# A bidirectional RWKV-7 scan on one core: another fixed order for solve steps, triangles and the attention group's output products

## The chip, the cores and the metric

The kernel runs on one core of a Trainium2 chip. The core has engines that work side by side, each through its own list of instructions: PE (TensorE: matrix products, with PEld as its weight load), DVE (VectorE), ACT (ScalarE), POOL (GpSimd) and SP (SyncE, which here only issues DMA transfers). SBUF is the on-chip memory, PSUM the banks into which PE writes. The metric is the device time of one execution in microseconds (us). The kernel before took a median of 2341.67 us over three runs, 2338.5 to 2344.6.

## What is computed

One layer of an encoder on x of shape 1 x 1024 x 1024, float32. In the reference, cut to what matters:

```
f = swiglu(rmsnorm(h), w_gate, w_up, w_down);  h = h + 0.5 * rmsnorm(f)
z = rmsnorm(h) @ w_in                        # attention q|k|v and RWKV r|k|v|decay|rate|gate
y_att  = dilated_attention(z[..., :1536]) * attn_out_g      # 8 heads of 64, normalised per head
y_rwkv = rwkv7(z[..., 1536:])                # 8 heads of 64, forward and backward
h = h + rmsnorm(concat(y_att, y_rwkv) @ w_out)
h = h + 0.5 * rmsnorm(swiglu(rmsnorm(h)))    # second feed-forward, D_FF = 2816

def step(state, r, w, k, v, kk, kka):        # rwkv7, per token, direction and head
    sa = state @ kk
    state = state * w - outer(sa, kka) + outer(v, k)
    return state, state @ r
```

The change concerns the stage in which the RWKV recurrence runs. The attention half of the product with w_out (512 of its 1024 rows) is worked in the same stage.

## The kernel before

Stages follow each other: the first feed-forward layer; projections and attention; preparation of the scan's first blocks beside the last projections; the scan; the finish of both halves with the rest of the output product; the second feed-forward layer. Where a feed-forward, projection or output product is made, float32 operands are split in a high and a low part, and three products are summed.

The recurrence is done in chunks of 64 tokens. The 1024 tokens are eight **blocks** of 128, two chunks each, and both directions and all eight heads are worked together. For block n there are these parts, each a Python generator or function that records instructions when it is advanced:

- *Preparation* (prep_parts). For each direction, `exps` makes two exponentials on ACT (L854, L855), and `times` scales keys, rates and receptances on DVE (L865 to L869, with a copy on ACT, L866). `triangles(d, i)` makes chunk i's products of keys with queries on PE (L876, tile lp) and returns `mask`, which cuts each of two halves to its triangle on DVE (L878, into lm). `turns(d)` transposes the scaled keys on PE (L888) and ACT copies them out (L891). `store` writes the triangles' diagonal pieces to DRAM (d_x) by SP (L897).
- *Solve* (solve_parts). It loads these pieces back in another layout as X and inverts them in 31 steps. A step is a product (L936, ttmp) and a subtraction (L938, Ti) on DVE, each dependent on the one before. A transpose on DVE (L941) ends it.
- *Merge* (merge_parts). Three groups of small products on PE (L953, L959, L966) with copies on ACT between (L954, L961 and L962, L968) build the inverse of twice the size. L953 needs the transpose of the solve.
- *Chain* (chain_parts). First come copies on ACT (L1002). Then, for each chunk in turn, products with the state and the values on PE (L1014, L1027, both xu), ACT copies between them (L1017 xs, L1029 uv), products into the new state st and the output y (L999), a copy of y (L1043), and the state's update by its decay on DVE (L1049, sv). Each chunk needs the state of the one before.
- *The attended output* (attended_parts) for eight tiles of 128 tokens: a row tile yat is loaded and scaled on DVE (L1271), transposed on PE (L1280, yq), split by ACT (L1282, yah) and DVE (L1286, yal). 24 products on PE (L1259, po) in four groups of six follow, and for each half of 512 columns ACT copies the sum (L1294, yao) and issues its store. The sums have one PSUM bank. The weights woh and wol are made by `out_weights` from eight loads into two raw buffers (wor).

The solve of block m+1 and the preparation of block m+2 run beside the merge and chain of block m. `scan` advances the generators in a written order. Then `in_order` ties each instruction of PE, DVE and ACT to the one recorded before it on its engine:

```
traced = self.nc.cur_bb.bb.instructions
...
for i in traced[start:]:
    if i.engine in self.ordered:
        if i.engine in last:
            self.tc.add_manual_dep(i, last[i.engine].name, ...)
        last[i.engine] = i
```

So within the scan those three engines follow the written order exactly. The lists of SP and POOL are left to the scheduler. An iteration of the scan over m is a *period* here, and it is cut at the first L953 of its merge.

Of the kernel before, what the change touches and what calls it, by code (L numbers as in the profile page):

```python
# [10 lines left out]
F32 = mybir.dt.float32  # L11
F32R = mybir.dt.float32r
# [151 lines left out]
class _Kernel:  # L164
# [903 lines left out]
    def scan(self, blk, NB, sp, sc, eo, pm, pp, pc, pe, homes, rs_a):  # L1068
# [4 lines left out]
        none = iter(())  # L1073
        go = lambda it, k=1: [next(it, None) for _ in range(k)]
        loaded = {n: {} for n in range(2, NB)}
        P, solves = {}, {}

        def loads(n, d):
            if n < NB:
                loaded[n][d] = self.prep_loads(n, d, sp)  # L1080

        def parts(n):
            if n < NB:
                got = self.prep_parts(n, sp, pp, homes[n % 3], loaded[n])
                blk[n], P[n] = got[0], got[1:]
                P[n][0](0)

        loads(2, 0)
        parts(2)
        WA = None  # L1090
        for m in range(NB):
            merge = self.merge_parts(m, blk[m], sc, pm)
            solve = solves.pop(m + 1, none)
            k = m + 2
            exps, times, triangles, turns, store = P.pop(k, (None,) * 5)
            go(merge)
            if exps:
                times(0)
                loads(k, 1)
            if WA:  # L1100
                go(rest)
            go(merge)
            chain = self.chain_parts(m, blk[m], sc, pc)
            go(chain)
            if exps:
                mask = triangles(0, 0)
            go(solve, 3)
            if WA:
                go(rest)
            if exps:  # L1110
                mask(0)
                mask(1)
            go(merge)
            go(chain)
            go(solve, 3)
            if exps:
                mask = triangles(0, 1)
                mask(0)
                go(solve)
                mask(1)  # L1120
                exps(1)
            if WA:
                go(rest)
            go(chain, 4)
            if WA:
                go(rest)
            if exps:
                times(1)
                loads(k + 1, 0)
            else:  # L1130
                go(solve, 4)
            go(chain)
            go(solve, 2)
            go(chain)
            if exps:
                turns(0)
                mask = triangles(1, 0)
            go(solve, 2)
            if exps:
                mask(0)  # L1140
                go(solve)
                mask(1)
            go(chain, 3)
            if exps:
                mask = triangles(1, 1)
            go(chain)
            go(solve, 2)
            if exps:
                mask(0)
                go(solve)  # L1150
                mask(1)
                store()
            go(chain)
            go(solve, 2)
            go(chain)
            if exps:
                turns(1)
                solves[k] = self.solve_parts(k, sp, blk[k])
                go(solves[k])
            if WA is None:  # L1160
                WA = self.out_weights(eo, 0, self.aog)
                rest = self.attended_parts(eo, sc, pe, list(range(NT)), WA, rs_a)
                go(rest)
            parts(k + 1)
            go(solve, 8)
            go(rest, 2)
            for _ in solve:
                pass
            if m >= 5:
# [58 lines left out]
    def finish_half(self, p, psum, half, x):  # L1228
        g2w = self.load_g2(p)
        for b in self.blocks[2 * half:2 * half + 2]:  # L1230
            sg = p.tile([128, FB], F32, name="f_sg", tag="f_sg", bufs=1)
            self.load(sg, self.sg_d[:, b * FB:(b + 1) * FB])
            for g in range(2):
                self.finish_unit(p, psum, b, g, x, g2w, sg)

    def out_weights(self, p, k0, gain=None, raw=None):

# [150 lines left out]
    def run(self):  # L1388
# [5 lines left out]
        with self.top as top:  # L1394
# [97 lines left out]
            blk = {}  # L1492
            for n, cts in enumerate(([], [8, 9, 10, 11])):
                blk[n] = self.prep(n, sp, pp, (R0, R1)[n])
                for _ in self.solve_parts(n, sp, blk[n]):
                    pass
# [12 lines left out]
            rs_a = self.rstd(eo, self.ss_a.rearrange("p a b -> p (a b)"), NT * H, 1.0 / HD, EPS)  # L1509
            self.scan(blk, NB, sp, sc, eo, pm, pp, pc, pe, (R0, R1, B0), rs_a)  # L1510
            s_sr.close()
            s_pr.close()

# [140 lines left out]
```

## Time and profile before

One execution was profiled. The scan runs from about 1248 to 1594 us of it.

| quantity | value |
|---|---|
| median of three runs | 2341.67 us (2338.5 to 2344.6) |
| the profiled execution, its own time | 2348.46 us |
| its span | 2346.7 us |
| mean granted TensorE clock | 0.963 |
| PE busy over the span | 2178.5 us, 93% |
| DVE busy | 1773.7 us, 76% |
| ACT busy | 1025.0 us, 44% |
| first merge's transposes (m = 0) begin | 1248.62 us |
| merges 1 to 7 begin | 1313.28, 1353.73, 1394.46, 1435.26, 1476.12, 1523.60, 1564.23 us |
| products for the second half of the output begin | 1593.83 us |

The median and the profiled execution differ by 6.8 us, so differences are formed within the one and then carried to the other. Busy shares are means over the whole program; in the scan neither PE nor DVE is full. The granted clock is the share of full speed at which PE was let run in a stretch. Group rows give the busy time, the mean duration of one in ns, and behind the second bar the idle time ahead with what ended it.

### The profile page before, as it was taken

What the parts mean: (1) busy time and instruction counts of PE and PEld (TensorE: products, weight loads), DVE (VectorE), ACT (ScalarE), POOL (GpSimd) and SP (SyncE); (2) the same over time, 40 slices, a digit from 0 to 9 for tenths busy, and PEclk for the clock granted to TensorE, in tenths of its full rate; (3) what the DMA queues carried; (4) which work ended last, traced back from release to release, by engine and by line L of the source; (5) the groups of instructions that cost most, each with busy time, mean ns of one, the idle gap of its engine ahead of it and who ended that gap; (6) DMA issues with size and microseconds to landing.
All of it is one profiled execution on the core that took longest, in us unless ns stands there. A gap on an engine that the chain in (4) does not pass through costs nothing. (4 is left out here: it accounts for less than half of the span.)

```text
span 2346.7 us, 41372 instructions
## 1 busy us (share of the span) xinstructions
PE 2178.5 (93%) x15556; PEld 1755.7 (75%) x15556; DVE 1773.7 (76%) x2893; ACT 1025.0 (44%) x1925; POOL 540.9 (23%) x673
## 2 busy tenths in 40 slices
PE   7999999999999998999997578779889999999998
PEld 5788888888877676777776466566678888887887
DVE  7999999865676344777767677646999999996566
ACT  5323323354676403676544444345442323235453
POOL 2344343400000011312212111122024443442000
PEclk9999999999999999999987889889989999999999
DMA  5354544486652515644377545436534544447665
GB/s 145 125 183 145 175 154 165 167 269 192 220 185 99 192 51 152 183 151 149 102 186 189 159 132 144 143 111 240 168 107 166 173 156 165 163 155 266 201 189 192
DMA packets 346700, 387.74 MB, mean 165 GB/s; under 512 B 73474, under 2 KB 249346, under 8 KB 346500
## 3 DMA queue, kind: packets, MB, share of 16 engines
q1 hardware_dynamic: 294928, 271.71, 38.2%
q0 software_dynamic: 31216, 100.73, 11.5%
q10 hardware_dynamic: 20356, 12.66, 1.8%
q8 instruction: 122, 2.00, 0.4%
q14 instruction: 78, 0.64, 0.1%
HBM read 258.06 MB, written 126.94 MB: 164 GB/s over the span
## 5 line engine op out<-in xcount | busy, mean ns | idle before, releaser
L81 PE MATMUL gu<-xh,wh 128*128 128x512 f32 x704 | 277.5, 394 | 4.6 <-ACT wh L186 4.5
L186 ACT ACTIVATE wh<-raw 128x512 fp32r<-128x512 f32 (+1 forms) x273 | 168.5, 628 | 250.2 <-DVE raw L62 93.4
L81 PE MATMUL gu<-xh,wl 128*128 128x512 f32 x704 | 276.1, 392 | 0.0
L81 PE MATMUL gu<-xl,wh 128*128 128x512 f32 x704 | 276.1, 392 | 0.0
L187 DVE TENSOR_TENSOR wl<-raw,wh 128x512 fp32r<-128x512 f32 (+1 forms) x273 | 272.4, 1001 | 4.8 <-ACT wh L186 3.9
L421 PE MATMUL pd<-gl,gwh 128*128 128x512 f32 x616 | 240.4, 390 | 2.6 <-DVE gl L187 2.6
L421 PE MATMUL pd<-gh,gwh 128*128 128x512 f32 x616 | 239.5, 390 | 0.6 <-DVE row L86 0.6
L421 PE MATMUL pd<-gh,gwl 128*128 128x512 f32 x616 | 239.8, 389 | 0.2 <-DVE gwl L187 0.2
L86 DVE TENSOR_TENSOR row<-gu,row 128x512 f32<-128x512 f32 x308 | 206.8, 683 | 25.2 <-PE gu L81 22.9
L116 POOL DMA_DIRECT2D d_hid<-row x154 | 85.0, 553 | 546.9 <-DVE row L114 531.9
L187 DVE TENSOR_TENSOR gwl<-graw,gwh 128x512 fp32r<-128x512 f32 (+2 forms) x187 | 117.5, 636 | 119.7 <-ACT gwh L186 117.6
L186 ACT ACTIVATE gwh<-graw 128x512 fp32r<-128x512 f32 (+2 forms) x187 | 103.3, 555 | 178.7 <-PE pd L421 148.2
L81 PEld LDWEIGHTS gu<-xh,wh 128*128 128x128 f32 x704 | 133.5, 190 | 33.7 <-ACT wh L186 5.6
L81 PEld LDWEIGHTS gu<-xh,wl 128*128 128x128 f32 x704 | 133.4, 189 | 28.1 <-DVE wl L187 0.2
L81 PEld LDWEIGHTS gu<-xl,wh 128*128 128x128 f32 x704 | 133.5, 190 | 27.5
L421 PEld LDWEIGHTS pd<-gl,gwh 128*128 128x128 f32 x616 | 115.6, 188 | 27.9 <-DVE gl L187 4.3
L421 PEld LDWEIGHTS pd<-gh,gwh 128*128 128x128 f32 x616 | 115.5, 188 | 25.3 <-DVE row L86 1.0
L421 PEld LDWEIGHTS pd<-gh,gwl 128*128 128x128 f32 x616 | 115.6, 188 | 24.6 <-DVE gwl L187 0.6
L187 DVE TENSOR_TENSOR gl<-raw,gh 128x512 fp32r<-128x512 f32 x160 | 112.5, 715 | 26.3 <-ACT gh L186 26.1
L94 ACT ACTIVATE row<-row 128x512 f32<-128x512 f32 x44 | 27.9, 634 | 213.9 <-DVE row L86 210.2
L186 ACT ACTIVATE gh<-raw 128x512 fp32r<-128x512 f32 x160 | 98.2, 622 | 44.7 <-DMA raw<-in_ffn_w_down_dram 24.8
L145 POOL TENSOR_TENSOR ws<-ws 128x512 f32<-128x512 f32 x88 | 114.7, 1304 | 1.2
(364 smaller groups left out, 5171.6 us busy)
## 6 DMA issues: line engine op xcount, KB each, us to landing
d_hid<-row POOLq DMA_DIRECT2D x154, 256.0 KB, 2.5
graw<-d_hid SPq DMA_DIRECT2D x132, 256.0 KB, 2.9
raw<-in_ffn_w_gate_dram SPq DMA_DIRECT2D x88, 256.0 KB, 3.2
raw<-in_ffn_w_up_dram SPq DMA_DIRECT2D x88, 256.0 KB, 3.3
ws<-in_ffn_w_down_dram SPq DMA_DIRECT2D x88, 256.0 KB, 4.1
d_ws<-ws POOLq DMA_DIRECT2D x88, 256.0 KB, 2.3
raw<-d_ws SPq DMA_DIRECT2D x88, 256.0 KB, 2.7
raw<-in_ffn_w_down_dram SPq DMA_DIRECT2D x66, 256.0 KB, 3.9
```

The costliest lines, as they stand in the source:

```text
L81: self.K.nc.tensor.matmul(ps, a[:, k, :], b[:, k, :], start=(k == 0 and i == 0), stop=(k == 3 and i == 2))
L86: add = lambda o, x: V.tensor_tensor(o, ps, x, op=OP.add)
L94: A.activation(y[:, 0], y[:, 0], AF.Silu)
L116: put = lambda n, y: G.dma_start(self.hid[n - 1, j // 2], y)
L145: G.tensor_tensor(o, a, b, op=OP.subtract)
L186: self.nc.scalar.activation(h, src, AF.Copy)
L187: (eng or self.nc.vector).tensor_tensor(l, src, h, op=OP.subtract)
L421: T.matmul(ps[x], a[:, ts], b, start=(m == 0 and k == 0), stop=(m == NM - 1 and k == 2))
```

## The change

No arithmetic is added or taken away, and tile shapes are the same. The order in which `scan` advances the generators is rewritten:

- The solve of block 1 moves from beside the last projections into the start of the scan. There it is mixed with the preparation of block 2 (the third block). Both directions of block 2's triangles now stand ahead of merge 0. Before, the first direction was under way in merge 0 and the second between its chunks.
- The attention group's reciprocal root (rstd) moves from ahead of the scan into iteration 0. A new generator `attended_weights` makes the output weights one pair at a time between the pieces of chain 0, in place of one run after it. The solve of block 2 begins there as well and has done 20 of its 31 steps by the end of iteration 0.
- In iterations 1 to 5 `times` of the first direction stands ahead of the merge. Each of two masks is followed by a solve step (`masks`). Of a tile's four groups of products only the last stays behind the merge, while the transposes and three groups stand behind the chain, ahead of the next merge. Iteration 3 takes one more whole tile; before, the additional tiles were in iterations 5 and 6.
- Iterations 6 and 7 are written out on their own. In 6, 13 solve steps stand ahead of the first chunk's state update on DVE, and the last tile's products stand ahead of merge 7.

```
+        def masks(mask, solve):
+            for par in range(2):
+                mask(par)
+                go(solve)
...
+        solve = self.solve_parts(1, sp, blk[1])
+        go(solve, 9)
         loads(2, 0)
         parts(2)
...
+        masks(triangles(1, 0), solve)
+        masks(triangles(1, 1), solve)
+        for _ in solve:
+            pass
+        store()
+
+        merge, chain, solve = begin(0)
+        weights = self.attended_weights(eo, W)
+        go(weights)
+        go(merge)
+        turns(1)
+        go(merge)
+        go(chain)
...
+        for m in range(1, NB - 2):
+            merge, chain, solve = begin(m)
             k = m + 2
...
+            times(0)
             go(merge)
+            loads(k, 1)
             go(merge)
             go(chain)
+            mask = triangles(0, 0)
+            go(solve, 4)
+            masks(mask, solve)
+            go(merge)
+            go(chain)
+            masks(triangles(0, 1), solve)
+            exps(1)
+            go(rest)
+            go(chain)
+            times(1)
+            loads(k + 1, 0)
+            go(chain, 4)
             go(solve, 3)
+            mask = triangles(1, 0)
             go(chain)
+            go(solve, 3)
+            masks(mask, solve)
+            go(chain, 5)
+            go(solve, 4)
+            go(chain)
+            mask = triangles(1, 1)
             go(solve, 2)
+            masks(mask, solve)
+            store()
+            solving(k)
+            go(rest)
+            turns(0)
+            turns(1)
             go(solve, 2)
+            go(rest, 4)
             parts(k + 1)
             for _ in solve:
                 pass
+            if m == 3:
+                go(rest, 6)
             blk.pop(m)
...
+    def attended_weights(self, p, W):
+
+        for k in range(4):
+            hl = []
+            for dh in range(2):
+                r = p.tile([128, 512], F32, name="wor", tag="wor", bufs=2)
+                self.load(r, self.io["w_out"][0][k * 128:(k + 1) * 128, dh * 512:(dh + 1) * 512])
...
+            yield
+            for h, l, r in hl:
+                self.nc.scalar.activation(h, r, AF.Copy, scale=self.aog[:, k:k + 1])
+                self.nc.vector.scalar_tensor_tensor(l, r, self.aog[:, k:k + 1], h, op0=OP.mult, op1=OP.subtract)
+            W.append([(h, l) for h, l, r in hl])
```

What this does to the engines' lists shows at three places. In the changed kernel the lines behind scan are 66 higher: L1325 is L1259 of before (po), L1346 is L1280 (yq), L1337 is L1271 (yat).

First, PE in a middle period, around its merge; po is a product of the attended output, lp a triangle, pa the merge. Before, each of the merge's three pieces has a group of six po behind it (one such group is shown):

```order
L888 MATMUL bp<-ident,bk 128x64 x16
L1280 MATMUL yq<-ident,yat 128x128 x4
L953 MATMUL pa<-ident,X 32x32 x64
L1259 MATMUL po<-woh,yah 128x512
L1259 MATMUL po<-wol,yah 128x512
L1259 MATMUL po<-woh,yal 128x512
```

In the changed kernel, the same place:

```order
L876 MATMUL lp<-pr,bk 128x128 x8
L1346 MATMUL yq<-ident,yat 128x128 x4
L888 MATMUL bp<-ident,bk 128x64 x32
L1325 MATMUL po<-woh,yah 128x512
L1325 MATMUL po<-wol,yah 128x512
L1325 MATMUL po<-woh,yal 128x512
L953 MATMUL pa<-ident,X 32x32 x64
L959 MATMUL pa<-X,lm 32x32 x32
L876 MATMUL lp<-pr,bk 128x128 x8
L966 MATMUL pa<-tt_12003,am 32x32 x32
```

The three po rows stand there six times in all, eighteen products, and all now precede the merge, whose pieces follow each other with triangles alone between them.

Second, DVE in a middle period: the masks of the first direction (lm) among the two operations of each solve step (ttmp, Ti). Before:

```order
L878 TENSOR_TENSOR lm<-lp,k_tri 128x512 x2
L936 TENSOR_TENSOR ttmp<-X,Ti 128x56
L938 TENSOR_TENSOR Ti<-Ti,ttmp 128x28x2
L936 TENSOR_TENSOR ttmp<-X,Ti 128x81
L938 TENSOR_TENSOR Ti<-Ti,ttmp 128x27x3
L936 TENSOR_TENSOR ttmp<-X,Ti 128x78
L938 TENSOR_TENSOR Ti<-Ti,ttmp 128x26x3
L878 TENSOR_TENSOR lm<-lp,k_tri 128x512
```

In the changed kernel:

```order
L878 TENSOR_TENSOR lm<-lp,k_tri 128x512
L936 TENSOR_TENSOR ttmp<-X,Ti 128x81
L938 TENSOR_TENSOR Ti<-Ti,ttmp 128x27x3
L878 TENSOR_TENSOR lm<-lp,k_tri 128x512
L936 TENSOR_TENSOR ttmp<-X,Ti 128x78
L938 TENSOR_TENSOR Ti<-Ti,ttmp 128x26x3
L878 TENSOR_TENSOR lm<-lp,k_tri 128x512
L936 TENSOR_TENSOR ttmp<-X,Ti 128x100
L938 TENSOR_TENSOR Ti<-Ti,ttmp 128x25x4
```

Where two masks stood in a row and three steps behind them, mask and step now take turns.

Third, PE at the start of the scan (vt is the transpose of the last values, L640, xu the first product of the chain). Before:

```order
L953 MATMUL pa<-ident,X 32x32 x64
L640 MATMUL vt<-ident,us 128x128 x8
L640 MATMUL vt<-ident,vrev 128x128 x8
L959 MATMUL pa<-X,lm 32x32 x32
L876 MATMUL lp<-pr,bk 128x128 x8
L966 MATMUL pa<-tt_12073,am 32x32 x32
```

In the changed kernel:

```order
L640 MATMUL vt<-ident,vrev 128x128 x4
L876 MATMUL lp<-pr,bk 128x128 x7
L888 MATMUL bp<-ident,bk 128x64 x16
L876 MATMUL lp<-pr,bk 128x128 x16
L953 MATMUL pa<-ident,X 32x32 x64
L888 MATMUL bp<-ident,bk 128x64 x16
L959 MATMUL pa<-X,lm 32x32 x32
L966 MATMUL pa<-tt_12003,am 32x32 x32
L1014 MATMUL xu<-sv,lm 64x64 x16
```

All triangles of the third block, both directions, now stand ahead of L953 of merge 0.

More of the change, by code (lines that the diff above doesn't have):

```diff
@@ L1091, in scan @@
-        for m in range(NB):
-            merge = self.merge_parts(m, blk[m], sc, pm)
-            solve = solves.pop(m + 1, none)
+        exps, times, triangles, turns, store = P.pop(2)
+        go(solve, 5)
+        times(0)
+        loads(2, 1)
+        go(solve, 4)
+        masks(triangles(0, 0), solve)
+        masks(triangles(0, 1), solve)
[3 more added lines that the diff above has]
+        times(1)
+        loads(3, 0)
+        masks(triangles(1, 0), solve)
+        masks(triangles(1, 1), solve)
@@ L1094, in scan @@
+        go(chain, 5)
+        go(solve, 8)
+        go(weights)
+        go(chain)
+        go(solve, 2)
+        rest = self.attended_parts(eo, sc, pe, list(range(NT)), W, rs_a)
+        go(weights)
+        go(rest)
+        parts(3)
+        go(rest)
+        go(solve, 3)
+        go(rest, 4)
+        go(solve, 3)
+        solves[2] = solve
+        blk.pop(0)
+        for m in range(1, NB - 2):
+            merge, chain, solve = begin(m)
             k = m + 2
-            exps, times, triangles, turns, store = P.pop(k, (None,) * 5)
+            exps, times, triangles, turns, store = P.pop(k)
+            times(0)
@@ L1096, in scan @@
             go(merge)
[L1097 to L1112, printed above, removed]
+            loads(k, 1)
             go(merge)
@@ L1134, in scan @@
[L1134 to L1137, printed above, removed]
-            go(solve, 2)
[L1139 to L1163, printed above, removed]
+            mask = triangles(0, 0)
+            go(solve, 4)
+            masks(mask, solve)
+            go(merge)
+            go(chain)
@@ L1173, in scan @@
+        go(solve, 3)
+        go(merge)
+        go(rest)
+        go(chain)
+        go(solve, 2)
+        go(chain, 5)
+        go(solve, 13)
+        go(chain)
+        go(chain, 5)
+        for _ in solve:
+            pass
+        go(chain)
+        for _ in rest:
+            pass
+        merge, chain, solve = begin(NB - 1)
+        go(merge, 2)
+        go(chain)
+        go(merge)
+        for _ in chain:
             pass
```

64 lines of the change are left out of this document (37 added, 27 removed).

## Prediction

> **What bounds the kernel now.** I first read the busy time by stretch, cut at the starts of the eight merges (the first transposes, L953). Columns: stretch (us), its length, then busy time with instruction counts on PE, PEld, DVE, ACT and POOL, the granted clock, the DMA share and GB/s.
>
> ```profile
> 1265.20:1313.28 48.08, 25.79 (x528) 23.14 (x532) 19.61 (x35) 23.70 (x40) 9.38 (x18) 0.68 0.62 165
> 1313.28:1353.73 40.45, 30.36 (x718) 25.46 (x718) 31.07 (x90) 18.98 (x34) 4.78 (x9) 0.88 0.56 152
> 1353.73:1394.46 40.73, 30.63 (x718) 25.52 (x718) 30.30 (x88) 18.37 (x33) 6.57 (x12) 0.88 0.53 144
> 1394.46:1435.26 40.80, 30.70 (x718) 25.53 (x718) 30.31 (x88) 18.38 (x33) 6.57 (x12) 0.88 0.52 144
> 1435.26:1476.12 40.86, 30.76 (x718) 25.60 (x719) 30.31 (x88) 18.38 (x33) 6.58 (x12) 0.88 0.54 143
> 1476.12:1523.60 47.48, 39.92 (x745) 32.03 (x745) 30.84 (x87) 18.31 (x33) 6.57 (x11) 0.88 0.45 135
> 1523.60:1564.23 40.63, 31.65 (x646) 25.31 (x645) 21.41 (x70) 13.78 (x25) 12.28 (x17) 0.92 0.48 147
> 1564.23:1594.29 30.06, 25.10 (x616) 19.18 (x616) 9.83 (x16) 20.43 (x37) 2.08 (x3) 0.89 0.15 46
> ```
>
> Four periods are alike, 40.45 to 40.86 us, and in each both PE and DVE are busy some 30 us: neither fills it. The fourth row is the period that I then followed along its chain of waits (start, length, what):
>
> ```profile
> 1394.46 1.93 PE pa L953 x128
> ...
> 1411.04 1.58 PE po L1259 x6
> ...
> 1421.28 0.69 DVE lm L878
> ...
> 1432.55 0.23 DVE Ti L938
> ...
> 1435.26 0.75 PE pa L953 x39
> ```
>
> PE carries the chain to 1421.28, DVE from there to the next merge. Each waits for the other once a period. The groups of the same period (busy, mean ns, then the idle time ahead and its releaser) price that:
>
> ```profile
> L878 DVE TENSOR_TENSOR lm<-lp,k_tri 128x512 f32<-128x512 f32 x8 | 5.4, 688 | 6.2 <-PE lp L876 6.2
> L1049 DVE TENSOR_TENSOR sv<-st,gc 64x512 f32<-64x512 f32 x4 | 2.7, 687 | 1.9 <-PE st L999 1.8
> L865 DVE SCALAR_TENSOR_TENSOR bk<-ka,th_w 128x512 f32<-128x512 f32 x3 | 2.1, 687 | 0.5 <-ACT th_w L855 0.5
> L938 DVE TENSOR_TENSOR Ti<-Ti,ttmp 128x126 f32<-128x126 f32 (+22 forms) x31 | 8.0, 257 | 1.1
> L953 PE MATMUL pa<-ident,X 32*32 32x32 f32 x130 | 2.2, 237 | 19.4 <-DVE gc L861 19.4
> ```
>
> DVE waits 6.2 + 1.9 + 0.5 = 8.6 us, so its own work with the latencies between dependent steps is 40.8 - 8.6 = 32.2 us. PE's 19.4 is two waits of 9.70, since the window catches both its ends; PE's work is then 40.8 - 9.7 - 0.4 = 30.7.
>
> **The long wait also cools PE.** Single rows around it (start, length, operation, and in brackets the wait ahead):
>
> ```profile
> 1394.45 1.93 PE L953 MATMUL pa<-ident,X 32*32 32x32 f32 x128 [9.70 <-DVE gc L861]
> 1396.90 0.63 PE L1259 MATMUL po<-wol,yah 128*128 128x512 f32 x1
> 1401.74 0.39 PE L1259 MATMUL po<-wol,yah 128*128 128x512 f32 x1
> 1415.96 1.16 PE L876 MATMUL lp<-pr,bk 64*128 64x128 f32 x14 [0.41 <-ACT bt L891]
> 1564.23 1.29 PE L953 MATMUL pa<-ident,X 32*32 32x32 f32 x128
> 1198.60 1.86 PE L876 MATMUL lp<-pr,bk 64*128 64x128 f32 x13 [2.86 <-DVE lm L878]
> ```
>
> After 9.70 us of waiting the transposes take 1.93 us, where a merge behind a full PE takes 1.29; a product takes 0.63 instead of 0.39. Pipelined, products follow each other at about 0.43 and 0.235 us. Without the cold start PE's work is some 28.7 us (0.64 on the transposes, about 6 x 0.2 on products, a little on L959).
>
> **The change, part by part.** No operation is added or removed; order is all that changes. *Steady period.* Before, DVE's triangle masks stand behind PE's attended products (po), and PE's merge stands behind DVE's solve steps. In the new order only one group of six po stays between merge and chain, eighteen come in one burst behind the chain, and each mask has a solve step behind it. So DVE gets its masks' inputs in turn, and its last steps run beside the burst. I take DVE as the bound. It saves about 0.5 by masks that stand directly behind a dependent step, as these rows show:
>
> ```profile
> 1406.22 0.26 DVE L938 TENSOR_TENSOR Ti<-Ti,ttmp 128x100 f32<-128x100 f32 x1
> 1406.40 0.68 DVE L878 TENSOR_TENSOR lm<-lp,k_tri 128x512 f32<-128x512 f32 x1
> 1432.80 0.21 DVE L936 TENSOR_TENSOR ttmp<-X,Ti 128x45 f32<-128x45 f32 x1
> 1433.04 0.20 DVE L938 TENSOR_TENSOR Ti<-Ti,ttmp 128x45 f32<-128x45 f32 x1
> ```
>
> The mask starts 0.18 after a step of 0.26, a dependent step 0.24 after one of 0.21: about 0.1 for each of five new places. Three waits stay: the scaling of the next block (times) needs exponentials that now stand on ACT behind the copy of a po group, 1.9 late by my tracing (twelve po at 0.235, the copy 0.6, the issue of its store 0.34, two exponentials 1.26, against 3.4 of steps and transpose on DVE); the state update 0.7; masks 0.4. Together 32.2 - 0.5 + 3.0 = **34.7** for m = 2, 4, 5. Unseen is how PE's pieces fall, so I bound it: 31.7 if all waits vanish (32.5 with a little left), 38.2 if the burst stays cold (below). I take the middle, near the DVE sum.
>
> *m = 1* has 11 solve steps left, since 20 are done in the opening. A step is two operations of some 0.29 with their latency (L938's row: (8.0 + 1.1)/31), so 20 x 0.6 = 12 leave DVE, and PE and ACT set about **32**, near the 30.06 of the last period, which is a merge and chain without solve. *m = 3* gets the one extra attended tile: transposes 0.66, copy 0.6, difference 0.69, 24 products 5.6, a wait for the copy of the single sum 0.7 and latencies, 8.7 in all: **43.4**. Before, m = 5 paid 47.48 - 40.86 = 6.6 for the same. *m = 6* has one tile where it had two, and its solve is spread: here
>
> ```profile
> 1541.74 1.41 DVE L1049 TENSOR_TENSOR sv<-st,gc 64x512 f32<-64x512 f32 x2 [9.51 <-PE st L999]
> ```
>
> is the wait of DVE for a PE full of po. 24 x 0.235 = 5.6 leave PE and 0.5 comes as a wait: **35.5**. *m = 7* stays **30**. From merge 1 on: 32 + 34.7 + 43.4 + 34.7 + 34.7 + 35.5 = 215.0 against 250.95, that is -36.0.
>
> *Opening.* Here the change costs. The third block's second direction stands now ahead of merge 0, and its inputs come late:
>
> ```profile
> 1264.08 0.52 SPq L182 DMA_DIRECT2D in<-d_rk  x1
> 1268.05 2.08 PE L876 MATMUL lp<-pr,bk 64*128 64x128 f32 x16
> 1273.93 2.10 PE L1014 MATMUL xu<-sv,lm 64*64 64x64 f32 x32
> 1292.45 1.39 DVE L1049 TENSOR_TENSOR sv<-st,gc 64x512 f32<-64x512 f32 x2 [0.87 <-PE st L999]
> 1295.85 1.33 ACT L1249 ACTIVATE woh<-wor,c_attn_out_g 128x512 fp32r<-128x512 f32 x2
> 1310.00 0.72 ACT L1249 ACTIVATE woh<-wor,c_attn_out_g 128x512 fp32r<-128x512 f32 x1 [0.44 <-DMA wor<-in_w_out_dram]
> in<-d_rk SPq DMA_DIRECT2D x2, 512.0 KB, 4.6
> ```
>
> The load is issued at 1264.08 behind stores of the values on SP and lands 4.6 later (last row, a median), at 1268.7. Four scalings of about 0.65 bring 1271; two groups of triangles at the cold 2.08 with four masks of 0.69 bring 1279. Merge 0, begun at 1276.6, needs three cold groups of 1.9 with ACT copies of 0.6, 1.8 and 1.2, so the first value product moves from 1273.93 to about 1287, +13. Both chunks follow cold: the second state update ends near 1305 instead of 1293.8. The weight conversions stood in a run of their own, 1295.85 to 1310.7. They now go between the chunks, but with two raw buffers the last two still wait for landings, to about 1315.5. Then the first attended tile (scale 0.65, transposes 1.1, copy 0.6, difference 0.7) and 18 cold po at 0.43 = 7.7: merge 1 at **1326** instead of 1313.28, +12.7. Bounds: 1318 if the conversions hide fully in the chain, 1332 if loads on SP slip again.
>
> The sum is -36.0 + 12.7 = -23.3 on a profiled execution of 2348.46 us (its span is 2346.7): 2325.2. The median of the runs shown lies 6.8 below that execution, so I predict **2319**.
>
> **What a page says of the cold burst.** The Trainium skill, "TensorE: Matmul & The Clock Gate", section "Part 1: The HAM clock gate (the "warmup" mystery)", puts the drop to half speed at an idle window of about 3.4 us. By that rule, none of my gaps (1.5 us at most) would cool PE and the forecast stands. The row at 1198.60 is slow after only 2.86 us, so the trace is stricter than the rule.
>
> **The rivals.** (1) *The clock drops at each burst.* 18 po at 0.43 instead of 0.235 cost 3.5, in six periods 21: 2319 + 21 = about **2340**, no change. For it: the slow row after a wait of 2.86, and that the burst waits for a difference on DVE behind solve steps. Against it: 9.7 shrinks to pieces that I trace at 1.5 or less. (2) *The opening is cheaper.* If weights and attended tile fit under the chain, merge 1 starts near 1317: **2310**. For it: ACT was busy only 23.70 of 48.08 there. Against it: loads, not ACT, paced the weights. (3) *X comes late.* Each solve starts from its masked products through DRAM:
>
> ```profile
> 1422.43 0.68 DVE L878 TENSOR_TENSOR lm<-lp,k_tri 128x512 f32<-128x512 f32 x1
> 1427.74 0.53 SPq L182 DMA_DIRECT2D X<-d_x  x1
> X<-d_x SPq DMA_DIRECT2D x1, 512.0 KB, 4.8
> ```
>
> From the mask's end (1423.1) to landing (1427.74 + 4.8) are 9.4 us. In the new order I count 10.4 from the last mask to the first step, with the load of the attended tile now ahead of the stores on SP. At 14 us, five periods grow by 3.6: **2337**, no change. (4) *Slower: the chain does not hide the triangles.* The bare merge and chain took 30.06. If the triangles (four groups of 1.1) and turns (1.4) find no gaps in it and the burst (4.4 + 0.7 for its copy) only adds, the period is 41, as before, nothing is won, and the opening's 12.7 stands: **2354**. It decides from a period of 38.9 on, where 23.3 are lost over the five and a half periods. For it: the transposes, products and copies of a chunk depend on one another. Against it: between 1406.80 and 1425 PE now runs triangles in just those gaps, with no wait over 0.41. That the order is not changed at all is excluded by the rows shown ahead.
>
> **How the numbers follow.** The forecast 0.62, cheaper opening 0.10, clock 0.14, late X 0.05, serial chain 0.09. 0.3% is 7 us, about what a measurement here can tell from none: faster means below 2334.6, so faster 0.72, same 0.19, slower 0.09. The range: best, opening -8 and three periods -2.2 each with m = 1 and 6 a little shorter, 2302; worst, opening +6 and four cold bursts, 2339. It leaves out the serial chain and the tail of the clock rival.
>
> **What will show it.** Merge 1 near 1326 and the next ones at 32, 34.7, 43.4, 34.7, 34.7, 35.5; DVE's idle ahead of L878 below 1 us a period instead of 6.2; no wait ahead of L953 over 2 us, and its transposes at 1.29; po of the burst 0.235 apart. I am wrong if PE is cold at the burst, if the first solve steps of a period wait for X, or if the opening ends far from 1326.

## The result, and the profile after

The changed kernel takes a median of 2355.5 us (2350.56 to 2357.91, four runs); the kernel before takes 2340.48 beside it. The ratio is 1.0059, with a 95% interval of 1.0037 to 1.0081: slower by 0.6%, where 2319 was forecast. Its profiled execution is 2355.06 us with a span of 2353.3. Runs of one kernel lie up to 16 us apart here, so below I compare ratios to the kernel before, measured on the same chip, and lengths of the scan in the profiles.

First the busy time by stretch of the changed kernel (columns as in the prediction). The first row runs from the last projection product to merge 1, the others from merge to merge.

```profile
1246.32:1325.00 78.68, 43.28 (x688) 36.10 (x687) 50.43 (x137) 29.67 (x50) 13.24 (x24) 0.63 0.61 164
1325.00:1360.27 35.27, 31.03 (x717) 25.66 (x716) 15.42 (x35) 17.74 (x32) 5.64 (x11) 0.95 0.52 132
1360.27:1400.02 39.75, 32.95 (x718) 27.38 (x717) 30.11 (x87) 18.54 (x34) 5.64 (x11) 0.91 0.57 161
1400.02:1451.36 51.34, 43.15 (x746) 34.88 (x745) 35.28 (x101) 20.92 (x38) 5.64 (x11) 0.83 0.54 149
1451.36:1491.40 40.04, 34.85 (x718) 29.00 (x717) 26.03 (x75) 17.74 (x32) 5.65 (x11) 0.83 0.45 123
1491.40:1529.58 38.18, 32.21 (x718) 26.49 (x717) 29.89 (x86) 17.34 (x32) 4.77 (x8) 0.91 0.48 132
1529.58:1568.31 38.73, 27.99 (x627) 23.04 (x626) 20.88 (x69) 12.56 (x23) 9.38 (x14) 0.87 0.47 141
```

Merge 1 comes at 1325.00, where 1326 was forecast. The six periods behind it take 243.3 us in sum where 215.0 was forecast, and 250.95 before. So the loop has become shorter, by 7.6 us where 36.0 were forecast, and the opening has become longer: 78.7 us from the last projection product to merge 1, where it was 64.6 before (1248.69 to 1313.28). Over the whole scan up to merge 7, PE is busy longer with the same instructions. Before:

```profile
1248.40:1564.23 315.83, 225.75 (x4923) 186.63 (x4921) 208.65 (x586) 134.75 (x238) 56.65 (x93) 0.84 0.54 152
```

After:

```profile
1246.03:1568.31 322.28, 245.75 (x4922) 202.55 (x4920) 208.29 (x591) 134.51 (x238) 50.21 (x91) 0.82 0.53 146
```

The stretch is 6.5 us longer. DVE's and ACT's busy times are unchanged, PE's grew by 20.0. The six periods alone, before and after:

```profile
1313.28:1564.23 250.95, 194.02 (x4253) 159.45 (x4253) 174.23 (x507) 106.21 (x191) 43.34 (x69) 0.88 0.51 144
1325.00:1568.31 243.31, 202.19 (x4235) 166.45 (x4234) 157.60 (x453) 104.84 (x188) 36.72 (x66) 0.88 0.50 140
```

In them PE stands still for 41.1 us where it was 56.9, but it is busy for 8.2 us more, and its mean granted clock is 0.88 as before; the rest of the 20.0 lies ahead of merge 1. How much of the growth is products that run slower, and how much waiting inside spans that the profile counts as busy, is not separated here. Now PE's timeline behind the chain of iteration 5 (start, length, operation, wait ahead and its releaser):

```profile
1515.33 1.16 PE L876 MATMUL lp<-pr,bk 64*128 64x128 f32 x16
...
1518.70 0.71 PE L888 MATMUL bp<-ident,bk 64*128 64x64 f32 x15 [1.42 <-DVE lm L878]
1519.78 1.36 PE L888 MATMUL bp<-ident,bk 64*128 64x64 f32 x16 [0.38 <-DVE lm L878]
1521.97 0.80 PE L1325 MATMUL po<-woh,yah 128*128 128x512 f32 x1 [0.83 <-DVE yal L1352]
1522.56 0.63 PE L1325 MATMUL po<-wol,yah 128*128 128x512 f32 x1
...
1527.98 0.50 PE L1325 MATMUL po<-woh,yah 128*128 128x512 f32 x1 [0.68 <-ACT yao L1360]
...
1529.58 1.29 PE L953 MATMUL pa<-ident,X 32*32 32x32 f32 x128
```

Three things are to be seen. The transposes of keys (bp) wait for the masks, because the last triangles and bp want four PSUM banks and there are three: the masks must free those of the triangles, and DVE does one of them behind a solve step. The first product of the burst waits for the difference yal, which stands on DVE behind the same masks and steps. Then twelve products come cold, 0.43 apart. From the end of the chain to the next merge 14.2 us pass. DVE has its part for that merge done 4.3 us before PE comes to it; its last transpose ends at 1525.29:

```profile
1524.21 1.08 DVE L941 STREAM_TRANSPOSE X<-Ti 128x512 f32<-128x512 f32 x1
```

And in the merge (iteration 3), where no po stands between the pieces any more:

```profile
1402.12 1.00 PE L959 MATMUL pa<-X,lm 32*32 32x32 f32 x50 [0.81 <-ACT tt L954]
...
1404.13 2.08 PE L876 MATMUL lp<-pr,bk 64*128 64x128 f32 x16
1406.14 1.92 PE L966 MATMUL pa<-tt,am 32*32 32x32 f32 x64
```

L959 starts warm, and the groups behind it take 2.08 and 1.92 us, the cold durations. The waits of PE by releaser, summed from merge 1 to merge 7 (total, times, longest), say where the 9.7 us went. Before:

```profile
PE pa L953 <- DVE gc L861: 38.8, 4, 9.7
PE po L1259 <- DVE yal L1286: 11.6, 3, 5.8
PE pa L959 <- issue: 0.8, 1, 0.8
```

After:

```profile
PE po L1325 <- DVE yal L1352: 8.0, 6, 2.3
PE bp L888 <- DVE lm L878: 5.8, 8, 1.4
PE po L1325 <- ACT yao L1360: 4.7, 7, 0.7
PE pa L959 <- ACT tt L954: 4.7, 6, 0.9
PE pa L959 <- issue: 4.2, 2, 3.5
```

Four long waits are gone, as the change intended. The short ones in these five rows, 29 of them, sum to 27.4 us.

### The profile page after: what moved, and what is told of

It reads as the page before. It is cut to its first block, busy times and chain, and to the rows that moved or that the text cites. A ratio compares the mean times of both kernels' runs of the same rounds, so it can differ in the third digit from the quotient of the medians.

```text
span 2353.3 us, 41391 instructions
## 1 busy us (share of the span) xinstructions
PE 2198.4 (93%) x15556; PEld 1771.9 (75%) x15556; DVE 1774.3 (75%) x2893; ACT 1025.0 (44%) x1925; POOL 538.5 (23%) x673
## 5 line engine op out<-in xcount | busy, mean ns | idle before, releaser
L81 PEld LDWEIGHTS gu<-xl,wh 128*128 128x128 f32 x704 | 133.2, 189 | 27.4
```

Source lines behind the costliest of these rows:

```text
L81: self.K.nc.tensor.matmul(ps, a[:, k, :], b[:, k, :], start=(k == 0 and i == 0), stop=(k == 3 and i == 2))
```

## The experiments

**The loop or the opening?** e1 keeps the changed opening and puts the loop of the kernel before behind it.

```
-        for m in range(1, NB - 2):
-            merge, chain, solve = begin(m)
...
+        for m in range(1, NB):
+            merge = self.merge_parts(m, blk[m], sc, pm)
+            solve = solves.pop(m + 1, iter(()))
...
```

> The changed opening (third block's triangles ahead of merge 0, weights between the pieces of chain 0, 20 steps of solve 2 done) with the loop of the kernel before from merge 1 on; the first attended tile's products go back into iteration 1. Theory A (the loss lies in the new loop: PE waits for masks and the attended difference behind the chain, and its burst of products runs cold): merge 1 near 1318, iteration 1 shorter than 40 because 11 solve steps are left (33 to 36), then 40.8 a period; the whole about 2338 to 2343, no different from before. Theory B (the loss is the opening's 12 us): merge 1 late by 5 or more and nothing won later, 2350 or more, near the changed kernel.

Measured: 2343.62 us, ratio 0.9999 (0.9988 to 1.0011). Iteration 1, with 11 steps left:

```profile
1311.74:1342.64 30.90, 30.16 (x717) 25.58 (x716) 22.44 (x56) 16.21 (x30) 5.06 (x11) 0.94 0.53 143
```

With the old loop the kernel is as fast as the kernel before. The edit does not part loop and opening cleanly, though: it also moves the first tile's products from the opening into iteration 1. So e1's opening takes 69.8 us (1241.93 to 1311.74) and not 78.7, and is paid back in iteration 1, which takes 30.9 instead of 40.5; its six periods sum to 243.8, as much as the changed kernel's 243.3. Against the kernel before, then, the loss stands ahead of merge 1, where the forecast had put it, and what failed is that the new loop won too little to pay for it. The next runs ask why.

**Is it PE's list behind the chain?** e2 transposes and splits the attended tile in the chain and puts bp behind two of the three po groups.

```
             go(chain)
+            go(rest)
             go(solve, 3)
             masks(mask, solve)
+            go(rest)
             go(chain, 5)
...
-            go(rest)
+            go(rest, 2)
             turns(0)
             turns(1)
             go(solve, 2)
-            go(rest, 4)
+            go(rest)
```

> The changed kernel, but in iterations 1 to 5 the attended tile is transposed and split early in the second chunk of the chain, and the transposes of keys (bp) stand behind two of the three po groups in place of ahead of all three. Nothing is left out. Theory A (behind the chain PE waits for masks of triangles that hold its PSUM banks, 0.4 to 1.4 us, and for the attended difference, 0.8 to 1.2, and is then cold for twelve products, 2.4): the stretch from the end of the chain to the next merge falls from 14.2 to 8.5-10, the period from 39 to 34-35.5, the whole by 18 to 27 us to 2328-2337. Theory C (ACT or the chain itself sets the period): the waits move to other places, period 38 to 40, the whole within 6 us of the changed kernel.

Measured: 2337.35 us, ratio 0.9974 (0.9963 to 0.9986): 18 us below the changed kernel by the medians (20 by the ratios), and faster than the kernel before. A row from the tail of iteration 4, and its whole period:

```profile
1470.19 0.71 PE L888 MATMUL bp<-ident,bk 64*128 64x64 f32 x15 [0.99 <-ACT bt L891]
...
1438.40:1473.79 35.39, 32.05 (x717) 27.28 (x716) 25.89 (x76) 17.87 (x32) 4.76 (x8) 0.90 0.47 123
```

The wait for the masks and the one for yal are gone, no product of the burst is cold, and from chain to merge 9.3 us pass in place of 13.8. The six periods sum to 228.4 us in its profile (243.3 without the edit). Theory A holds, at the weak end of its size; iteration 2 still takes 38.0.

**ACT's list?** e3 puts the next block's exponentials ahead of the attended sums' copies.

```
             turns(1)
+            parts(k + 1)
             go(solve, 2)
             go(rest, 4)
-            parts(k + 1)
```

> The changed kernel, but the next block's exponentials stand on ACT ahead of the copies of the attended sums, so that DVE can scale the next block while PE works its burst. Theory A (PE's list is the bound): DVE's wait for the exponential (3.9 us in iteration 5) vanishes, the period stays within 1 us, the whole 2350 to 2357. Theory C (ACT's list sets the period): 2 to 4 us a period in five periods, the whole 2336 to 2346.

Measured: 2359.03 us, ratio 1.0066 (1.004 to 1.0092). No gain: DVE's wait for the exponential goes, and in iteration 5 a wait of 5.6 us for X stands in its place. So ACT's list alone does not set the period; what it would cost with X early no run separates.

**The clock.** e4 makes the last chunk's triangles twice, so that PE works where it waited.

```
-            mask = triangles(1, 1)
+            mask = triangles(1, 1, 2)
...
-            for pr in range(4):
+            for pr in list(range(4)) * times:
```

> The changed kernel, but the last chunk's triangles of each of iterations 1 to 5 are made twice on PE, with the same result: 1.1 us of PE work a period that stands where PE otherwise waits for the masks. Theory A with the clock as part of it: the work fills the wait ahead of bp, the burst's first twelve products come at 0.235 in place of 0.43, the period falls by 1 to 2.5 us, the whole 2343 to 2351. If the clock does not hang on that gap: bp waits no less (DVE's masks come after the second product group), the period grows by 0 to 1.1, the whole 2355 to 2361.

Measured: 2347.08 us, ratio 1.0021 (1.0006 to 1.0036). With 1.1 us of work *added* to five periods the kernel is 8 us faster by the medians (9 by the ratios). Its profile cannot show where, for the profiled execution was the slowest of the ten (2357.54 us): only iterations 1 and 2 are shorter there than in the changed kernel (34.4 and 35.9 for 35.3 and 39.8), and the six periods sum to 248.9. In iteration 2:

```profile
1390.45 0.71 PE L888 MATMUL bp<-ident,bk 64*128 64x64 f32 x15 [0.53 <-DVE lm L878]
...
1393.71 0.50 PE L1325 MATMUL po<-woh,yah 128*128 128x512 f32 x1 [1.17 <-DVE yal L1352]
```

The wait ahead of bp shrank from 1.33 to 0.53 us, and the burst behind the same 1.17 us wait for yal stays warm. Iterations 3 and 5 still have cold products, so the filling does not always do it. That more work made the kernel faster is shown by the medians; that it did so by the clock is seen in single bursts like this one. The traces of e10 and e16 below show what decides.

**The next bound.** e5 adds e3's edit to e2.

```
             solving(k)
+            parts(k + 1)
             go(rest, 2)
```

> As e2_early_yq, and in addition the next block's exponentials stand on ACT ahead of the copies of the attended sums. In e2 DVE waited 5.8 us for the exponential and 3.8 us for X behind it, since SP's list has a load that waits for the scaled block ahead of the load of X. Theory A (once PE's waits behind the chain are gone, the waits of DVE at a period's start reach the merge through the triangles): merges of 12-14 us fall to 10-12, the whole 2325 to 2333. If the merge is long because PE's clock falls within it, not because of DVE: the merge stays at 11.5-14 and the whole within 4 us of e2 (2333 to 2341).

Measured: 2345.05 us, ratio 0.9997 (0.9984 to 1.0011): 8 us worse than e2, outside both expectations. Iteration 5, on SP, DVE and PE:

```profile
1480.63 0.38 SPq L182 DMA_DIRECT2D in<-d_rk  x1
1481.19 1.04 SPq L182 DMA_DIRECT2D X<-d_x  x1
1487.21 0.19 DVE L936 TENSOR_TENSOR ttmp<-X,Ti 128x31 f32<-128x31 f32 x1 [6.01 <-DMA X<-d_x]
1489.86 2.07 PE L876 MATMUL lp<-pr,bk 64*128 64x128 f32 x14 [4.41 <-DVE lm L878]
```

SP's list has the next block's load of `in` ahead of X. It waits for its buffer, which DVE frees at about 1480.6 by the last scaling that reads `in`. X lands at 1487, the first solve steps and the mask behind them are late, and the second triangle group waits for the mask's PSUM bank. e6 puts one po group back into the merge, between L953 and L959.

```
             loads(k, 1)
+            go(rest)
             go(merge)
...
             go(solve, 2)
-            go(rest)
```

> As e5_yq_exps, but one of the three po groups of the burst goes back between the first and the second piece of the merge, as in the kernel before; two groups stay behind the chain. If the merge's small products with ACT copies between them cool PE: L959, L966 and the triangles in the merge stay at 1.2 us in place of 1.9 to 2.1, the merge takes 10.5-11.5 with twelve po in it while the tail shrinks by 1.4 to about 8, the period 33-34.5, the whole 2318 to 2328. If not: the merge grows by the 1.4 that the tail loses, the whole as e5.

Measured: 2340.56 us, ratio 0.9983 (0.9969 to 0.9998). The same wait for X (6.3 us) hides what the po group does, so e6 alone decides nothing. Then SP's list was tied to the written order, in e10 on e5 and in e11 on e6.

```
-        self.ordered = (E.PE, E.DVE, E.Activation)
+        self.ordered = (E.PE, E.DVE, E.Activation, E.SP)
```

> As e5_yq_exps, with SP's transfers in the scan tied to the written order too, so that the load of X stands ahead of the next block's loads, which wait for their buffers. In e5 the first solve step of a period waited 6.0 us for X, a product group of the merge 4.4 us behind it, and the merge took 16 us. If the queue's order is the cause: X is issued 4 to 6 us earlier, the merges take 10 to 12, the whole falls by 12 to 22 us against e5 (2323 to 2333). If X is late by the round trip through DRAM itself: DVE still waits 3 us or more for it and the whole stays within 6 us of e5 (2339 to 2351).

> As e6_po_merge, with SP's transfers in the written order. If X's place in SP's list was what hid the gain of the po group in the merge: period 33 to 35.5, the whole 2318 to 2330 and 0 to 6 us below e10. If the round trip is too long for a period of 34 us: 2336 or more.

Measured: e10 2332.7 us, ratio 0.9933 (0.9908 to 0.9959); e11 2333.53, 0.9943 (0.9925 to 0.9962), between its two ranges. So X's place in SP's list cost 12 us by the medians (15 by the ratios), at the weak end of what was expected. DVE's waits for X, four in the six periods, fall from 27.9 to 11.1 us in sum. And the po group in the merge is worth nothing that can be measured. Iterations 1, 2 and 5 of e10:

```profile
1318.05:1350.80 32.75, 29.08 (x717) 24.40 (x716) 17.93 (x39) 18.25 (x33) 5.64 (x11) 1.00 0.49 137
1350.80:1385.11 34.31, 29.21 (x717) 24.41 (x716) 27.47 (x84) 18.12 (x33) 4.77 (x8) 1.00 0.62 171
...
1470.39:1506.71 36.32, 33.14 (x716) 28.07 (x716) 29.91 (x86) 17.22 (x31) 6.57 (x11) 0.86 0.54 151
```

At a granted clock of 1.00 the periods are 32.75 and 34.31. These are the 32 and 34.7 of the prediction, reached where three things are met that it took for granted: fewer waits behind the chain, X earlier, a warm PE. All six periods sum to 227.2 all the same, where 215.0 was forecast: iterations 3 and 6 take 49.36 and 38.53, and in 4 and 5 the clock falls.

**The kernel before, once more.** e7 is that kernel unchanged.

> The kernel before once more, unchanged, for a second profile. The first one has 1248.3 us ahead of the scan's first merge, where the changed kernels have 1240 to 1247 with the same instructions; from the last projection product to merge 7 it has 315.9. If the scan is steady, this stretch is again 315 to 317 and the stages around it differ by up to 8 us.

Measured: 2348.98 us, and 315.91 us from 1245.80 to merge 7 at 1561.71. In these two executions the scan repeats to 0.1 us, while the stages ahead of it and behind it differ by 2 to 3 us.

**The opening.** e8 moves the reciprocal root ahead of everything, converts weights earlier and works the first tile in the chain; e12 is the same with the root behind the first merge piece.

```
+        rs_a = self.rstd(eo, self.ss_a.rearrange("p a b -> p (a b)"), NT * H, 1.0 / HD, EPS)
         solve = self.solve_parts(1, sp, blk[1])
...
         go(merge)
         turns(1)
+        go(weights)
         go(merge)
...
```

> The changed kernel with its opening written otherwise: the reciprocal root ahead of everything, the first weights loaded with the third block and converted where ACT and DVE wait (from 1268 us on), the first attended tile between the pieces of chain 0, its yq early; the iterations unchanged. If late weights set the opening's end: the wait of 10 us ahead of yq vanishes, merge 1 comes 7 to 12 us earlier after the last projection product, the whole 2343 to 2349. If the chain itself sets it: 0 to 3 us, 2352 to 2356.

> As e8_opening, but the reciprocal root stands behind the first merge piece instead of ahead of everything (there its two table loads and the wait of DVE held the first merge back by 16 us), and the first weights are converted among the last triangles. If late weights set the opening's end in the changed kernel: merge 1 comes 9 to 12 us earlier, the whole 2343 to 2348. If not: 2352 to 2357.

Measured: e8 2357.7 us, ratio 1.0049 (1.0032 to 1.0066), nothing won. In it PE waited for block 2's exponential, which stood behind the root's table loads on ACT:

```profile
1260.76 1.28 ACT L216 ACT_TABLE_LOAD   x1
1272.78 2.47 PE L876 MATMUL lp<-pr,bk 64*128 64x128 f32 x18 [12.71 <-ACT e L854]
```

e12: 2344.07 us, ratio 0.9989 (0.9973 to 1.0004), 11 us below the changed kernel by the medians (16 by the ratios). From the last projection product to merge 1:

```profile
1248.95:1319.08 70.13, 42.47 (x686) 35.61 (x687) 45.16 (x123) 29.16 (x49) 13.25 (x25) 0.63 0.66 174
```

70.1 us instead of 78.7, and the wait of 10 us ahead of yq is gone. Late weights did set the opening's end, as far as one edit shows it that also moves the first tile's transposes into the chain.

**Both together.** e13 is e11's loop with e12's opening, e16 is e10's loop with it.

> e11's iterations with e12's opening. If the parts add up: 8 to 12 us below e11, 2308 to 2321, faster than the kernel before by 20 us or more. If the opening's gain is eaten by the first iterations (X of block 2, loads of block 3): within 4 us of e11.

> e10's iterations with e12's opening, so that the opening's effect is seen without the po group in the merge. If e12's 11 us carry over: 2319 to 2326. If the first iterations take it back, as in e13 where iteration 1 took 37.2: 2326 to 2334.

Measured: e13 2329.82 us, ratio 0.9911 (0.9881 to 0.994); e16 2325.72, 0.9916 (0.9898 to 0.9934). The opening takes 4 us off e11 and 7 off e10 by the medians (7 and 4 by the ratios), not its 11 to 16, so part of it is given back; in one profile of each, e13's iteration 1 takes 37.2 us where e11's took 31.8. The intervals don't tell e13 and e16 apart. Both beat the kernel before by about 0.85%.

**Why the clock falls in the merge.** e15 adds five unused full-size products a period in the merge's two waits for ACT; e17 is e16 with the same.

```
+            for _ in range(k):
+                T.matmul(ps.rearrange("p a b -> p (a b)"), w[:, 0:128], w, start=True, stop=True)
...
             loads(k, 1)
+            triangles("ahead", (0, 0, W[0][0][0], 2))
             go(merge)
...
+            triangles("ahead", (0, 1, W[0][0][0], 3))
             masks(mask, solve)
             go(merge)
```

> As e10_e5_sp, with five full-size products (128x128 by 128x512, their result is written over by the triangles and not used) a period in the merge's two waits of 0.7 us for ACT, two ahead of L959 and three ahead of L966. In e10 the merge takes 9.3 us in iterations 1 and 2, where the granted clock is 1.00, and 12 in 4 and 5, where it falls to 0.50 inside the merge. If small products with short waits are what lets the clock fall: the merges of 4 and 5 fall to 9.3-9.8, clock 1.00, the whole 6 to 12 us below e10 (2321 to 2327). If the fall comes from the wait ahead of L953 or from further back: merges of 12 or more, the whole 0 to 5 us above e10.

> e16 with e15's added products. If both hold: 2312 to 2320. If the added products only cost: as e16 plus up to 5.

Measured: e15 2335.71 us, ratio 0.9948 (0.9926 to 0.997), not below e10; e17 2322.27, 0.9905 (0.9884 to 0.9925), the lowest of all, though its interval overlaps that of e16; it lies between its two ranges. In e15, iteration 4 and a row in it:

```profile
1439.22:1479.11 39.89, 32.44 (x722) 26.50 (x722) 25.89 (x76) 17.88 (x32) 4.77 (x8) 0.91 0.41 117
...
1446.33 0.54 PE L970 MATMUL pa<-X,lm 32*32 32x32 f32 x13 [4.14 <-issue]
```

Iteration 5 runs warm (34.66 us at 1.00), and in iteration 4 PE stops for 4.14 us in the middle of a group, for nothing that this view shows. In e16, without added products, both iterations are warm, 34.17 and 34.16 us; the second:

```profile
1461.03:1495.19 34.16, 29.21 (x716) 24.40 (x716) 29.81 (x86) 17.22 (x31) 6.54 (x11) 1.00 0.56 160
```

The loop is e10's, where the same two iterations were at 0.90 and 0.86. So the added products decide nothing. What decides shows when the traces are cut where the granted clock changes. In each of the 17 traces of this case these places are whole multiples of 3.41 us apart, a grid that stands still within an execution and lies elsewhere in the next. The merge of iteration 5 begins at 1470.39 in e10 and at 1461.03 in e16, with the same waits ahead of its first two pieces, 1.32 and 0.68 us. Cut on each one's own grid (columns as before, so the third number is PE's busy time), e10:

```profile
1469.57:1472.98 3.41, 1.91 (x166) 1.80 (x168) 3.22 (x6) 1.20 (x2) 1.80 (x3) 1.00 0.60 191
1472.98:1476.39 3.41, 3.41 (x76) 3.12 (x70) 2.14 (x9) 2.40 (x5) 0.00 (x0) 0.50 1.08 310
...
1479.81:1483.22 3.41, 3.41 (x19) 2.37 (x20) 3.34 (x10) 2.33 (x4) 0.00 (x0) 0.50 0.00 0
1483.22:1486.63 3.41, 3.41 (x95) 3.03 (x94) 3.24 (x10) 1.85 (x4) 0.00 (x0) 1.00 0.22 82
```

And e16:

```profile
1460.81:1464.22 3.41, 2.51 (x194) 2.36 (x194) 2.92 (x8) 1.20 (x2) 1.79 (x3) 1.00 0.89 287
1464.22:1467.64 3.42, 2.41 (x81) 2.07 (x82) 3.15 (x13) 2.97 (x5) 0.00 (x0) 1.00 0.88 250
```

Where the grid leaves PE only 1.91 us of work in one stretch, the next stretch runs at half clock; where it shares the waits out between two, the clock stays. Counted from 1235 to 1600 us of all traces, half clock followed each of the 114 stretches at full clock in which PE was busy for less than 1.5 us, 1 of the 1056 with more than 2.6, and 74 of the 227 between. So it is the waits that fall into one stretch which count together, and whether waits of this size cool PE depends on where the grid happens to lie. This is counted over the traces; no run set it on purpose.

## Why the prediction was wrong

*The opening: right.* Forecast 1326, measured 1325.0, by the working given: merge 0 at 1273.62 (1276.6 forecast) and the last weights late, then the tile's transposes behind them. Counted from the end of the last projection product, merge 1 moved by 14.1 us where 12.7 was forecast; that product ended 2.4 us earlier in this execution, so that the hit to 1 us is in part luck. The rows:

```profile
1312.17 1.33 ACT L1298 ACTIVATE woh<-wor,c_attn_out_g 128x512 fp32r<-128x512 f32 x2 [5.22 <-DMA wor<-in_w_out_dram]
1315.00 1.11 PE L1346 MATMUL yq<-ident,yat 128*128 128x128 f32 x4 [9.96 <-DVE yat L1337]
```

*The steady period: wrong.* The step that failed is "I take DVE as the bound", with 34.7 for it. Measured are 39.75, 40.04 and 38.18; 38.2 had been set as the bound if the burst stays cold. DVE's own sum came out well: its transpose for the next merge ends 36.2, 35.6 and 33.9 us after the merge before began. But PE comes to that merge only 3.6 to 4.4 us later, so PE is the bound. I had put PE's list at 28.7 us warm and taken its waits for hidden. In iteration 5 PE itself waits 5.7 us in seven pieces, the profile's waits summed from merge to merge, and twelve cold products add 12 x 0.2 = 2.4. That makes 36.8 of 38.2; the rest lies in spans that I have not placed. I missed that bp needs the banks that the masks free, though the three buffers of PSUM were in the code, and I left yal where the order has it without asking what stands ahead of it on DVE. e2 takes just these waits away and the kernel goes from 1.0059 to 0.9974. There three merges wait for DVE, 1.3 us each: only then does DVE bound a period. (Two slips in the sum are too small to matter: the parts of the 1.9 for the late exponentials add up to 1.6, and 2325.2 less 6.8 is 2318.4.)

*"None of my gaps would cool PE": wrong.* No wait between chain and merge is above 1.42 us in iteration 5, and its burst is cold. On that execution's grid the waits for masks and yal leave PE 1.59 us of work in one stretch, and two stretches at half clock follow:

```profile
1516.78:1520.19 3.41, 1.59 (x22) 1.01 (x22) 3.20 (x10) 1.34 (x3) 0.34 (x1) 1.00 0.82 194
1520.19:1523.60 3.41, 2.58 (x19) 2.12 (x20) 3.04 (x13) 1.40 (x3) 0.00 (x0) 0.50 1.05 299
...
1527.02:1530.43 3.41, 2.73 (x108) 1.90 (x108) 0.00 (x0) 0.59 (x1) 0.00 (x0) 1.00 0.86 231
```

By the Trainium skill, "TensorE: Matmul & The Clock Gate", section "HAM oscillation — how this bites in real kernels", gaps above some 3.4 us are the ones to avoid. This trace disagrees: short waits in a row sufficed here, and the measurement decides. Rival 1 had this mechanism, at 21 us. What the clock cost in all is not separated: PE's busy time grew by 8.2 us in the six periods, and the mean granted clock, which the forecast had counted on to rise, stayed at 0.88.

*m = 3 and m = 6.* 43.4 was forecast for the extra tile and 51.34 came: the same waits and cold products twice. 35.5 was forecast for m = 6 and 38.73 came. m = 1 took 35.27 for 32. Summed, the periods missed by 28.3 us.

*From the profile to the median.* I took 6.8 us off because the kernel before's profiled execution lay that far above its median. For the changed kernel the profiled execution (2355.06) lies at the median. That carry was noise: the profiled execution lies 10.5 us above the median in e4 and 9.6 below it in e11. It accounts for 6.8 of the 36.5 us by which the forecast missed; with the 28.3 of the periods and the 1.4 of the opening, all of it is told.

*The rivals.* The fourth, 2354 us, has the time and the side, and its condition was met: the three steady periods are 39.3 us in the mean where it set 38.9. But its mechanism was only half right. The triangles do find their place in the chain, which takes 14.5 to 15 us now; it is behind the chain that PE stands. The third, late X, shows in the changed kernel in two periods (waits of 1.4 us in iteration 2 and 6.3 in iteration 6; what they cost is not worked out). In e5, with PE's waits and those for the exponentials gone, it cost 12 us through the queue on SP: e10 gained these with the loads themselves unchanged. The 11.1 us of waits for X left in e10 may be the round trip's.

## What to carry to other kernels

When one long wait of an engine is dissolved by a reordering, add up the short waits that the new order leaves on the same engine, with the buffers that its next work must get free, before calling another engine the bound. For PE's clock it is not the longest wait that counts in these traces, but how little work is left in one stretch of 3.41 us. A queue that the written order does not cover (SP here) must be looked at too: a load that waits for its buffer holds back the load that is due. And a median's distance from one profiled execution is not a constant to be carried over.

## What the runs showed that was not expected

PE works a long time at half speed without a wait. In the stretches of e10's iteration 5 shown with e16 it was busy without a pause from 1472.98 on, and the granted clock stayed at 0.50 for three stretches, 10.2 us. It came back only some 3.5 us into the po group that began at 1479.67. Before that stood the merge's 32x32 products and the triangles. That small products do not count as full work for the clock would fit, but it was not shown.

The other is "issue", time in which PE waits for nothing that these views show, in the middle of its groups of small products, mostly the merge's. Before, from merge 1 to merge 7, it was 0.8 us, once; after, the rows with that releaser sum to 8.8 us, up to 3.5 at a time, and up to 4.14 in e15. The DMA view shows what it is. A transfer of 16 KB on a queue of the kind "instruction", q8, ran from 1443.96 to 1444.90 us in the middle of e15's long stop, which ended at 1446.33 (transfers, MB, share of the DMA engines):

```profile
q8 instruction: 1, 0.02, 2.4%
```

In the 17 traces, from 1235 to 1600 us, there are 94 such waits of PE, and each ended 1.2 to 1.6 us after a landing on q8, though only one lands in some 8 us. By this count PE waits there for instructions that are still being fetched, though the view does not say for which engine q8 fetches. In the kernel before PE had stood still for 9.7 us ahead of most merges; that they were fetched in that time would explain its 0.8, and is a guess.
